# A hybrid mixer layer on one core: later adaLN columns summed on VectorE during S5's inputs, the out projection of two token blocks under the last branch, and a shorter norm chain

## The chip, the cores and the metric

The kernel runs on one core of one Trainium2 chip. The metric is the device time of one launch in microseconds (us). TensorE (PE) does matmuls, VectorE (DVE), ScalarE (ACT) and GpSimd (POOL) elementwise work, and all DMAs of this kernel are issued from SyncE's queue (SP), in that queue's order.

## What is computed

One layer of a hybrid backbone: 512 latent and 256 context tokens of width 1024. Three mixers (HGRN2, gated DeltaNet, S5) run on one norm of the input; their outputs are projected, gated, added and projected out, and an MLP follows. The six adaLN vectors `ml[0]` to `ml[5]` are columns of one product with `ada_w`. The first two are needed at the start, `ml[2]` to `ml[4]` only behind the mixers, `ml[5]` at the end. Cut to what matters:

```python
ml = split(silu(c) @ ada_w + ada_b, 6)
pl = split(modulate(rmsnorm(xl, norm1_w), ml[0], ml[1]) @ w_in, ...)
ya, yb, ycc = hgrn2(...) @ w_ba, deltanet(...) @ w_bb, s5(...) @ w_bc
xl = xl + ml[2] * ((g_a * ya + g_b * yb + g_c * ycc) @ w_o)      # g: sigmoid gates of pl
xl = xl + ml[5] * (square(relu(modulate(rmsnorm(xl, norm2_w), ml[3], ml[4]) @ w1)) @ w2)
return rmsnorm(xl, final_norm_w)
```

All is float32. A product is made of three TensorE matmuls on two parts of each operand.

## The kernel before

Each operand of a product is split into a high part `hi`, rounded by ScalarE (L225, L238), and a low part `lo`, the rest, by VectorE (L226, L239) or GpSimd; `mm3` (L245 to L248) adds three matmuls. Weights stream through `W`: half-megabyte loads into three `raw` buffers, then two buffers each of `hi` and `lo`. A load can be issued when the split of the load three before it is done. SyncE issues in order, so a DMA that waits holds up all behind it.

The code is written as generators, `weave` runs a main one and a filler by a plan, and a scheduler then lists each engine's order from the trace of the program. After that the order of each engine is fixed: a matmul that waits holds all matmuls behind it.

The stages, by the times of the profile: start and first adaLN vectors to 56 us; S5's input projection to 98; `state_in` (L338 to L374), which makes S5's inputs, to 147; the S5 scan on GpSimd from 147 on, beside HGRN2; two pairs of DeltaNet heads (545 to 705 and 717 to 905) with fillers; the rest of branch c to 945; branch b to 990; the out projection with norms to 1042; the MLP to 1395; the last norms.

`state_in` takes eight groups. Each spreads a 16-wide factor over 128 columns in six elementwise operations (L338 to L347), five of the groups on GpSimd and three on VectorE, transposes the result on TensorE (L365), copies it on ScalarE (L367), multiplies with the columns `U` (L370) and copies into the scan's state `sv` (L372 to L374). `U` is written to DRAM in `s5du` by four blocks and read back in another layout, one load for two groups.

`ada_rest(j, pool)` makes one of `ml[2]` to `ml[5]`. Eight matrices of 128x1024 are loaded into `raw`, scaled by a column of `silu(c)` on ScalarE (L1290) and added up on GpSimd (L1291). Eight matmuls of one column (L1297) sum over partitions, and VectorE adds the bias (L1298). j = 2, 3 and 4 run as fillers of the second DeltaNet pair, together with `branch("a")`; j = 5 runs in the MLP's first half.

`branch(n, ...)` goes over eight blocks of output columns: a gate, a weight block (`W.load`), 12 matmuls, `(gate + 1) * p` on VectorE (L1384), the add of the branches so far, loaded from `mg` (L1388), and `last(b, g)`. For branch b `last` splits the merged block into `gh` and `gl`. Between the blocks `resident` loads and splits one block of `w_out` with GpSimd's help. The out projection runs behind that, for four blocks of 128 tokens and two halves of columns, each into a `pj` bank of PSUM, followed by gate and residual (L1487, L1488) and `norm`. `norm` takes squares with sums on ScalarE (L1495), 13 VectorE steps on 128x1 (L1496, L1497 and `rsqrt`, L183 to L188), and the scaling of `x1` by VectorE (L1513). After transposes the modulation of eight column blocks is VectorE's (L1521).

## Time and profile before

| | |
|---|---|
| median of 3 runs | 1406.12 us (1405.9 to 1409.2) |
| profiled execution | 1412.48 us |
| its span, first to last instruction | 1410.8 us |
| busy: TensorE, VectorE, ScalarE, GpSimd | 90%, 63%, 34%, 28% of the span |
| mean granted TensorE clock | 0.956 of full speed |
| DMA | 161.31 MB, mean 114 GB/s |

The page gives busy times, the windows give them for a stretch, and the timeline gives each instruction with the idle time of its engine before it and what released it. A row names the line, the engine, the operation, the output and inputs by the program's names, and the shapes.

### The profile page before, as it was taken

What the parts mean: (1) busy time and instruction counts of PE and PEld (TensorE: products, weight loads), DVE (VectorE), ACT (ScalarE), POOL (GpSimd) and SP (SyncE); (2) the same over time, 40 slices, a digit from 0 to 9 for tenths busy, and PEclk for the clock granted to TensorE, in tenths of its full rate; (3) what the DMA queues carried; (4) which work ended last, traced back from release to release, by engine and by line L of the source; (5) the groups of instructions that cost most, each with busy time, mean ns of one, the idle gap of its engine ahead of it and who ended that gap; (6) DMA issues with size and microseconds to landing.
All of it is one profiled execution on the core that took longest, in us unless ns stands there. A gap on an engine that the chain in (4) does not pass through costs nothing. (4 is left out here: it accounts for less than half of the span.)

```text
span 1410.8 us, 18360 instructions
## 1 busy us (share of the span) xinstructions
PE 1276.2 (90%) x6829; PEld 1047.0 (74%) x6829; DVE 886.7 (63%) x1705; ACT 482.5 (34%) x879; POOL 391.1 (28%) x510
## 2 busy tenths in 40 slices
PE   7788999999998898899976889976999999999995
PEld 2367777888787786798866788754777888888884
DVE  6744487866779668897559766437766422544236
ACT  3426313433334355222252432223234422244222
POOL 0255799997005620000004630004004000000002
PEclk9898999999999899999988989989999999999998
DMA  8773442738847674924565775788226333332321
GB/s 292 122 148 55 56 62 38 110 51 66 109 65 124 74 166 129 101 46 68 117 160 183 225 151 95 161 184 245 78 60 182 117 96 98 90 105 90 105 90 61
DMA packets 182266, 161.31 MB, mean 114 GB/s; under 512 B 24800, under 2 KB 152480, under 8 KB 182176
## 3 DMA queue, kind: packets, MB, share of 16 engines
q1 hardware_dynamic: 182176, 160.14, 52.8%
q8 instruction: 54, 0.88, 0.3%
q14 instruction: 36, 0.29, 0.1%
HBM read 141.24 MB, written 18.87 MB: 113 GB/s over the span
## 5 line engine op out<-in xcount | busy, mean ns | idle before, releaser
L226 DVE TENSOR_TENSOR lo<-raw,hi 128x1024 fp32r<-128x1024 f32 (+1 forms) x161 | 189.9, 1180 | 260.2 <-ACT hi L225 259.9
L225 ACT ACTIVATE hi<-raw 128x1024 fp32r<-128x1024 f32 (+1 forms) x161 | 157.5, 979 | 398.3 <-PE pj L247 228.2
L246 PE MATMUL pj<-hh,hi 128*128 128x512 f32 (+1 forms) x520 | 216.3, 416 | 16.5 <-ACT hi L225 11.5
L248 PE MATMUL pj<-hh,lo 128*128 128x512 f32 (+1 forms) x520 | 213.8, 411 | 1.0 <-DVE lo L226 1.0
L247 PE MATMUL pj<-hl,hi 128*128 128x512 f32 (+1 forms) x520 | 213.3, 410 | 0.8 <-POOL hl L1148 0.8
L247 PE MATMUL pj<-hc,hi 128*128 128x512 f32 (+2 forms) x536 | 187.4, 350 | 1.7 <-DVE hc L239 0.8
L246 PE MATMUL pj<-h,hi 128*128 128x512 f32 (+1 forms) x304 | 117.1, 386 | 12.6 <-ACT hi L225 11.5
L246 PEld LDWEIGHTS pj<-hh,hi 128*128 128x128 f32 (+1 forms) x520 | 101.2, 195 | 35.6 <-ACT hi L225 12.5
L248 PE MATMUL pj<-h,lo 128*128 128x512 f32 (+1 forms) x304 | 116.5, 384 | 3.6 <-DVE lo L226 3.3
L247 PEld LDWEIGHTS pj<-hl,hi 128*128 128x128 f32 (+1 forms) x520 | 101.1, 194 | 21.1 <-POOL hl L1148 2.4
L248 PEld LDWEIGHTS pj<-hh,lo 128*128 128x128 f32 (+1 forms) x520 | 100.4, 193 | 21.9 <-DVE lo L226 2.1
L247 PEld LDWEIGHTS pj<-hc,hi 128*128 128x128 f32 (+1 forms) x536 | 101.9, 190 | 16.4 <-DVE hc L239 1.6
L1584 POOL TENSOR_TENSOR xn<-x,row 128x512 f32<-128x512 f32 x8 | 10.4, 1301 | 313.4 <-DVE x L1488 307.6
L246 PE MATMUL pj<-hc,hi 128*128 128x256 f32 (+2 forms) x264 | 86.0, 326 | 11.3 <-ACT hi L225 7.1
L248 PE MATMUL pj<-hc,lo 128*128 128x256 f32 (+2 forms) x264 | 84.9, 322 | 5.0 <-DVE lo L226 5.0
L1291 POOL TENSOR_TENSOR s<-s,raw 128x1024 f32<-128x1024 f32 x21 | 51.3, 2444 | 113.8 <-DMA mg<-fg 81.4
L246 PEld LDWEIGHTS pj<-h,hi 128*128 128x128 f32 x304 | 57.8, 191 | 26.5 <-ACT hi L225 14.9
L248 PEld LDWEIGHTS pj<-h,lo 128*128 128x128 f32 x304 | 57.7, 190 | 17.8 <-DVE lo L226 7.2
L246 PEld LDWEIGHTS pj<-hc,hi 128*128 128x128 f32 (+1 forms) x264 | 50.8, 193 | 15.9 <-ACT hi L225 7.5
L248 PEld LDWEIGHTS pj<-hc,lo 128*128 128x128 f32 (+1 forms) x264 | 50.7, 192 | 8.9 <-DVE lo L226 5.9
L382 POOL TENSOR_TENSOR sw<-sp,sv 128x64 f32<-128x64 f32 x94 | 50.7, 540 | 22.9 <-ACT sv L373 15.6
L239 POOL TENSOR_TENSOR act<-raw,act 128x1024 fp32r<-128x1024 f32 x8 | 19.2, 2395 | 127.0 <-ACT act L238 127.0
(535 smaller groups left out, 2760.3 us busy)
## 6 DMA issues: line engine op xcount, KB each, us to landing
raw<-in_w_in SPq DMA_DIRECT2D x72, 512.0 KB
raw<-in_w_ff SPq DMA_DIRECT2D x64, 512.0 KB
raw<-in_ada_w SPq DMA_DIRECT2D x40, 512.0 KB
dg<-fg SPq DMA_DIRECT2D x16, 256.0 KB
fg<-dg SPq DMA_DIRECT2D x16, 256.0 KB
mg<-fg SPq DMA_DIRECT2D x16, 256.0 KB
fg<-mg SPq DMA_DIRECT2D x16, 256.0 KB
raw<-in_w_out SPq DMA_DIRECT2D x8, 512.0 KB
```

Source lines behind the costliest of these rows:

```text
L225: K.nc.scalar.activation(hi, w, AF.Copy)
L226: (engine or K.nc.vector).tensor_tensor(lo, w, hi.bitcast(FT), op=OP.subtract)
L239: (engine or K.nc.vector).tensor_tensor(lo, x, hi.bitcast(FT), op=OP.subtract)
L246: nc.tensor.matmul(out, wh, xh, start=start, stop=False)
L247: nc.tensor.matmul(out, wh, xl, start=False, stop=False)
L248: nc.tensor.matmul(out, wl, xh, start=False, stop=stop)
L382: e.tensor_tensor(t[:, 1], aa[:, 1], ap(x, 96 * G, [[-96 * G, 2], [96, G]]), op=OP.mult)
L1291: nc.gpsimd.tensor_tensor(acc, acc, w, op=OP.add)
L1584: nc.gpsimd.tensor_tensor(t[:, s], x1[i][:, s], fw[:, s], op=OP.mult)
```

## The change

Three things change.

1. `ada_rest` for j = 2, 3 and 4 leaves the second pair's fillers and is run by `ada_gates` in steps of `state_in`, which is now a generator. Loads are 1 MB into the two buffers of the tag `nt`; the first matrix is scaled by ScalarE, the seven others are scaled and added by one VectorE instruction each. The column sums, the bias and the write of `drow` follow there. The last of the three runs on in `chain(mix(hgrn2_in(0), taps, ...))`. The plan and the filler list of the second pair are new.
2. The out projection of the first two token blocks is issued in `last` of branch b, for the block before, into the `tr` and `mm` banks. `w_out` goes through the two `xn` buffers instead of `raw`, and `x1` is loaded from block 4 on.
3. The norm chain has 9 steps instead of 13 (a factor of -1/256 goes into `mod2` and into the final weight), the scaling of `x1` and two in four modulations are ScalarE's. j = 5 uses a `raw` tile for each matrix and one more step.

```diff
+    def ada_rest(j, acc, fetch, engine):
+        kt = 0
+        while kt < 8:
+            two = fetch()
+            n = two.shape[1]
+            k.dma(two, ada_w[128 * kt:128 * (kt + n), 1024 * j:1024 * j + 1024].rearrange("(x p) m -> p x m", p=128))
+            for i in range(n):
+                w, c = two[:, i], cs[:, kt + i, 0:1]
+                if not kt + i:
+                    nc.scalar.activation(acc, w, AF.Copy, scale=c)
+                elif engine is v:
+                    v.scalar_tensor_tensor(acc, w, c, acc, op0=OP.mult, op1=OP.add)
+                else:
+                    nc.scalar.activation(w, w, AF.Copy, scale=c)
+                    engine.tensor_tensor(acc, acc, w, op=OP.add)
+            kt += n
+            if kt % 2 == 0:
+                yield
+        yield
...
+    def ada_gates():
+        done = iter(())
+        for j in (2, 3, 4):
+            g = ada_rest(j, k.t("s4", [128, 1024]), lambda: k.t("nt", [128, 2, 1024]), v)
+            for i in range(4):
+                next(g)
+                if i == 1:
+                    for _ in done:
+                        pass
+                yield
+            done = g
+        yield done
...
-    s5.state_in()
+    ada = ada_gates()
+    for _ in s5.state_in():
+        next(ada)
     s5.scan()
+    for last_sums in ada:
+        pass
...
-    for _ in chain(mix(hgrn2_in(0), taps), gates(0, range(0, 1))):
+    for _ in chain(mix(hgrn2_in(0), taps, last_sums), gates(0, range(0, 1))):
...
-    weave(pair(1), chain(gates(1, range(2, 3)), mix(gates(1, range(3, 5)), gates(1, range(5, 6))), mix(branch("a", w_ba, range(8), last=save(mg[0])), chain(gates(1, range(6, 8)), ada_rest(2, s4), mix(ada_rest(3, s4), ada_rest(4, s4)))), branch("c", w_bc, (), scale=0.25, prev=mg[0], last=save(mg[1]))), (7, 11), (8, 6), (8, 4), (4, 6), (21, 8))
+    weave(pair(1), chain(gates(1, range(2, 6)), mix(branch("a", w_ba, range(8), last=save(mg[0])), gates(1, range(6, 8))), branch("c", w_bc, (), scale=0.25, prev=mg[0], last=save(mg[1]))), (7, 6), (5, 4), (12, 4), (21, 4))
...
+    def merged(b, g):
+        split_act(k, gh[:, b], gl[:, b], g)
+        if b:
+            for i in range(2):
+                for h in range(2):
+                    project_out(first[i][h], i, h, b - 1)
+
+    for b, _ in enumerate(branch("b", w_bb, range(8), prev=mg[1], last=merged)):
+        wo += resident(w_out, 128 * b, 1, lambda shape: k.t("xn", shape), nc.gpsimd)
...
-        v.tensor_tensor(st[:, i, 2:3], st[:, i, 0:1], st[:, i, 1:2], op=OP.add)
-        v.tensor_scalar(st[:, i, 2:3], st[:, i, 2:3], 1.0 / 1024, EPS, op0=OP.mult, op1=OP.add)
-        rsqrt(v, st[:, i, 4:5], st[:, i, 2:3], st[:, i, 3:4])
-        return t, st[:, i, 4:5]
+        x, y, z = st[:, i, 2:3], st[:, i, 3:4], st[:, i, 4:5]
+        v.tensor_scalar(x, st[:, i, 0:1], st[:, i, 1:2], 1024 * EPS, op0=OP.add, op1=OP.add)
+        v.tensor_scalar(z.bitcast(I32), x.bitcast(I32), 1, None, op0=OP.logical_shift_right)
+        v.tensor_scalar(y.bitcast(I32), z.bitcast(I32), -1.0, 1597463007.0, op0=OP.mult, op1=OP.add)
+        for c in (3.0, 12.0, 768.0):
+            v.tensor_scalar(z, y, y, x, op0=OP.mult, op1=OP.mult)
+            v.scalar_tensor_tensor(y, z, c, y, op0=OP.subtract, op1=OP.mult)
+        return t, y
...
-        v.tensor_scalar(t, x1[i], r, None, op0=OP.mult)
+        nc.scalar.activation(t, x1[i], AF.Copy, scale=r)
```

What this does to the order of instructions is read at three places. The first is SyncE's queue in S5's inputs; `s` with the source `s5du` is a load of U, `s5du` as a target a write of it. Before:

```order
L63 DMA s_100_831<-s5du_567 128x8x96
L63 DMA s5dul<-s_98_824 1024x1x64
L63 DMA s_117_909<-s5du_568 128x8x96
L63 DMA s5du_570<-s_98_824 8x16x768
L63 DMA s_134_987<-s5du_569 128x8x96
L63 DMA s_151_1065<-s5du_570 128x8x96
L63 DMA raw_1946<-in_w_in 128x8x128
```

Now, from the third of these rows on:

```order
L62 DMA s_120_920<-s5du_568 128x8x96
L62 DMA s5du_570<-s_98_826 8x16x768
L62 DMA nt_960<-in_ada_w 128x2x1024
L62 DMA nt_1002<-in_ada_w 128x2x1024
L62 DMA s_139_1006<-s5du_569 128x8x96
L62 DMA nt_1047<-in_ada_w 128x2x1024
L62 DMA nt_1089<-in_ada_w 128x2x1024
L62 DMA drow<-r_1106 8x128
L62 DMA s_161_1109<-s5du_570 128x8x96
L62 DMA nt_1149<-in_ada_w 128x2x1024
L62 DMA nt_1191<-in_ada_w 128x2x1024
L62 DMA raw_2035<-in_w_in 128x8x128
```

The third and fourth load of U now stand behind two and four loads of 1 MB, and the fourth behind the write of `drow` too, which waits for the first column sum. VectorE in the same place, before, at its last group of `state_in`:

```order
L338 TENSOR_TENSOR s_160_1105<-sp_428,s_76_429 128x512
L339 TENSOR_TENSOR s_127_950<-sp_428,s_76_429 128x512
L341 TENSOR_TENSOR s_160_1105<-sp_428,s_76_429 128x512
L340 TENSOR_TENSOR s_126_949<-s_126_949,s_127_950 128x512
L342 TENSOR_TENSOR s_127_950<-sp_428,s_76_429 128x512
L347 TENSOR_TENSOR s_126_949<-s_126_949,s_127_950 128x512
```

Now, from the first sum of j = 3 to the end of the last group of `state_in`:

```order
L1191 SCALAR_TENSOR_TENSOR s_148_1046<-nt_1047,cs,s_148_1046 128x1024
L337 TENSOR_TENSOR s_171_1153<-sp_428,s_76_429 128x512
L340 TENSOR_TENSOR s_171_1153<-sp_428,s_76_429 128x512
L1191 SCALAR_TENSOR_TENSOR s_148_1046<-nt_1089,cs,s_148_1046 128x1024 x2
L1191 SCALAR_TENSOR_TENSOR s_148_1046<-nt_1149,cs,s_148_1046 128x1024
L338 TENSOR_TENSOR s_172_1154<-sp_428,s_76_429 128x512
L1191 SCALAR_TENSOR_TENSOR s_148_1046<-nt_1149,cs,s_148_1046 128x1024
L339 TENSOR_TENSOR s_171_1153<-s_171_1153,s_172_1154 128x512
L1191 SCALAR_TENSOR_TENSOR s_148_1046<-nt_1191,cs,s_148_1046 128x1024
L341 TENSOR_TENSOR s_172_1154<-sp_428,s_76_429 128x512
L1191 SCALAR_TENSOR_TENSOR s_148_1046<-nt_1191,cs,s_148_1046 128x1024
L346 TENSOR_TENSOR s_171_1153<-s_171_1153,s_172_1154 128x512
```

All seven sums of j = 3 stand ahead of the end of the last spread, six of them between its operations. The third place is TensorE in branch b. Before, its 12 matmuls of a block (`h` with a `hi` or `lo`) follow those of the block before, and the first matmul of the out projection (`act`, `gh`) stands in the last block:

```order
L248 MATMUL pj_8378<-h_1363_8155,lo_8375 128x512
L246 MATMUL pj_8411<-h_1363_8155,hi_8407 128x512
L247 MATMUL pj_8411<-h_1363_8155,hi_8407 128x512
L246 MATMUL pj_8450<-act_8201,gh 128x512
L247 MATMUL pj_8450<-act_8202,gh 128x512
L248 MATMUL pj_8411<-h_1363_8155,lo_8408 128x512
```

Now, at the end of one block and the start of the next:

```order
L247 MATMUL pj_8263<-h_1355_8115,lo_8260 128x512
L245 MATMUL tr_8111<-act_8251,gh 128x512
L246 MATMUL tr_8111<-act_8252,gh 128x512
L247 MATMUL tr_8111<-act_8251,gl 128x512
...
L245 MATMUL mm_8114<-act_8251,gh 128x512
L246 MATMUL mm_8114<-act_8252,gh 128x512
L247 MATMUL mm_8114<-act_8251,gl 128x512
L245 MATMUL pj_8308<-h_1355_8115,hi_8304 128x512
```

From the third block on, 12 matmuls of the out projection stand behind the 12 of each block (six of them left out in the fence).

## Rows read from the trace of the kernel before

**Rows 1.** The page, parts 1 and 5: busy time, share, count; groups.

```profile
PE 1276.2 (90%) x6829; PEld 1047.0 (74%) x6829; DVE 886.7 (63%) x1705; ACT 482.5 (34%) x879; POOL 391.1 (28%) x510
...
L226 DVE TENSOR_TENSOR lo<-raw,hi 128x1024 fp32r<-128x1024 f32 (+1 forms) x161 | 189.9, 1180 | 260.2 <-ACT hi L225 259.9
...
L1291 POOL TENSOR_TENSOR s<-s,raw 128x1024 f32<-128x1024 f32 x21 | 51.3, 2444 | 113.8 <-DMA mg<-fg 81.4
```

**Rows 2.** Windows: length, busy PE, PEld, DVE, ACT, POOL; PE clock, DMA share, GB/s.

```profile
0.00:56.00 56.00, 38.11 (x129) 11.23 (x129) 36.84 (x206) 20.15 (x40) 2.09 (x8) 0.96 0.78 247
98.00:147.00 49.00, 38.47 (x249) 33.89 (x248) 25.59 (x24) 26.81 (x68) 23.48 (x18) 0.90 0.38 67
739.00:840.00 101.00, 81.00 (x522) 73.33 (x522) 82.48 (x124) 38.40 (x46) 54.05 (x25) 0.90 0.69 189
910.00:940.00 30.00, 18.68 (x67) 14.09 (x66) 8.91 (x12) 6.53 (x10) 0.00 (x0) 0.83 0.91 184
920.00:930.00 10.00, 5.58 (x20) 4.19 (x18) 0.00 (x0) 0.00 (x0) 0.00 (x0) 0.84 0.90 70
945.00:983.00 38.00, 25.07 (x87) 17.04 (x86) 26.28 (x26) 13.86 (x21) 16.42 (x7) 0.91 0.74 229
```

**Rows 3.** Timeline of TensorE, pair 1: start, us, instruction, idle before and releaser.

```profile
746.95 0.79 PE L248 MATMUL pj<-hc,lo 128*128 128x512 f32 x1 [4.10 <-DVE lo L226]
...
789.75 1.84 PE L1297 MATMUL att<-one,s 128*128 128x1 f32 x16
...
825.99 0.50 PE L246 MATMUL pj<-hh,hi 128*128 128x512 f32 x1 [2.64 <-ACT hi L225]
```

**Rows 4.** Timeline of VectorE in pair 1, four column scalings twice.

```profile
741.95 3.15 DVE L844 TENSOR_SCALAR s<-upper,gu 128x128 f32<-128x128 f32 x4
...
751.62 1.08 DVE L844 TENSOR_SCALAR s<-upper,gu 128x128 f32<-128x128 f32 x4
```

**Rows 5.** Timeline of TensorE at the end of branch c.

```profile
917.44 0.50 PE L246 MATMUL pj<-hh,hi 128*128 128x512 f32 x1 [3.72 <-ACT hi L225]
...
932.65 0.80 PE L246 MATMUL pj<-hc,hi 128*128 128x512 f32 x1 [7.07 <-ACT hi L225]
```

**Rows 6.** Timeline of TensorE in branch b.

```profile
954.60 0.50 PE L246 MATMUL pj<-h,hi 128*128 128x512 f32 x1 [1.69 <-ACT hi L225]
...
957.27 0.39 PE L247 MATMUL pj<-h,hi 128*128 128x512 f32 x1
957.50 0.39 PE L248 MATMUL pj<-h,lo 128*128 128x512 f32 x1
...
982.81 0.50 PE L246 MATMUL pj<-h,hi 128*128 128x512 f32 x1 [1.15 <-ACT hi L225]
```

**Rows 7.** Timeline of VectorE in branch b, the merge add.

```profile
951.37 0.69 DVE L1388 TENSOR_TENSOR fg<-fg,fg 128x512 f32<-128x512 f32 x1 [2.60 <-DMA fg<-mg]
...
956.50 2.67 DVE L1388 TENSOR_TENSOR fg<-fg,fg 128x512 f32<-128x512 f32 x1 [1.24 <-DMA fg<-mg]
```

**Rows 8.** Timeline of VectorE, two steps of the last norm chain.

```profile
1403.51 0.15 DVE L1497 TENSOR_SCALAR st<-st 128x1 f32<-128x1 f32 x1
1403.70 0.15 DVE L183 TENSOR_SCALAR st<-st 128x1 int32<-128x1 int32 x1
```

**Rows 9.** Timeline of TensorE, VectorE and GpSimd in S5's inputs.

```profile
104.86 3.70 PE L370 MATMUL mm<-s,s 128*128 128x96 f32 x16 [6.01 <-DMA s<-s5du]
...
115.92 1.66 DVE L338 TENSOR_TENSOR s<-sp,s 128x512 f32<-128x512 f32 x1 [9.73 <-PE tr L365]
...
123.89 1.43 DVE L347 TENSOR_TENSOR s<-s,s 128x512 f32<-128x512 f32 x1
...
112.58 1.06 POOL L338 TENSOR_TENSOR s<-sp,s 128x512 f32<-128x512 f32 x1
...
130.09 1.60 POOL L347 TENSOR_TENSOR s<-s,s 128x512 f32<-128x512 f32 x1
...
147.26 0.35 POOL L382 TENSOR_TENSOR sw<-sp,sv 128x64 f32<-128x64 f32 x1 [15.57 <-ACT sv L373]
```

More of the change, by code (lines that the diff above doesn't have):

```diff
@@ L1174, in project @@
         return res if len(res) > 1 else res[0]
+    mod2 = consts.tile([128, 4, 8], FT, name="mod2")
+    drow = k.d("drow", [2, 1024])
+    def ada_rest(j, acc, fetch, engine):
[17 more added lines that the diff above has]
+        yield
+        m = mod2[:, j - 2]
+        p = k.p("att", [128, 8])
+        for b in range(8):
+            nc.tensor.matmul(p[:, b:b + 1], acc[:, 128 * b:128 * b + 128], k.one, start=True, stop=True)
+        v.tensor_tensor(m, p, at["ada_b"][:, 8 * j:8 * j + 8], op=OP.add)
+        if j == 4:
+            v.scalar_tensor_tensor(m, m, 1.0, at["n2"], op0=OP.add, op1=OP.mult)
+            v.tensor_scalar(m, m, -1.0 / 256, None, op0=OP.mult)
+        if j in (2, 5):
+            if j == 2:
+                v.tensor_scalar(m, m, 0.5, None, op0=OP.mult)
+            p = k.p("att", [8, 128])
+            nc.tensor.transpose(p, m, k.ident)
+            r = consts.tile([8, 128], FT, name=f"r{j}")
+            nc.scalar.activation(r, p, AF.Copy)
+            k.dma(drow[j // 3].rearrange("(b n) -> b n", b=8), r)
+        yield
+    def ada_gates():
[7 more added lines that the diff above has]
+                        pass
+                yield
+            done = g
+        yield done
     def silu2(out, p, x=None):
@@ L1473, in resident, with project_out @@
         return res
-    wo = []
-    for b, _ in enumerate(branch("b", w_bb, range(8), prev=mg[1], last=lambda b, g: split_act(k, gh[:, b], gl[:, b], g))):
-        wo += resident(w_out, 128 * b, 1, nc.gpsimd)
-    x1 = [k.t("x1", [128, 1024]) for _ in range(4)]
-    for i in range(4):
-        k.dma(x1[i], x[128 * i:128 * i + 128])
+    wo, first = [], [[k.p(n, [128, 512]) for _ in range(2)] for n in ("tr", "mm")]
+    x1 = []
+    def project_out(p, i, h, kt):
+        s, w = slice(128 * i, 128 * i + 128), slice(512 * h, 512 * h + 512)
+        mm3(nc, p, gh[:, kt, s], gl[:, kt, s], wo[kt][0][:, w], wo[kt][1][:, w], kt == 0, kt == 7)
+    def merged(b, g):
[6 more added lines that the diff above has]
+        wo += resident(w_out, 128 * b, 1, lambda shape: k.t("xn", shape), nc.gpsimd)
+        if b >= 4:
+            i = b - 4
+            x1.append(k.t("x1", [128, 1024]))
+            with k.queued(nc.sync):
+                k.dma(x1[i], x[128 * i:128 * i + 128])
+    for i in range(2):
+        for h in range(2):
+            project_out(first[i][h], i, h, 7)
     G2 = row(drow[0])
@@ L1539, in hybrid_block @@
         for f in range(16):
-            if not half and 4 <= f < 9:
+            if not half and 4 <= f < 10:
                 next(last_ada)
```

58 lines of the change are left out of this document (17 added, 41 removed).

## The prediction

> **What bounds the kernel now.** I read the page's busy shares first. TensorE is busy 90% of the span [rows 1], so what can be gained is the 10% in which it stands, and the stretches in which it runs at a lower granted clock. The windows [rows 2] say where these are: each gives TensorE's busy time, its granted clock (as a share of 2.4 GHz) and the DMA share. What the diff touches are four stretches: 98 to 147 us (S5's inputs, 38.47 busy of 49), 739 to 840 (second pair of DeltaNet heads, 81.00 of 101), 910 to 940 (last blocks of branch c, 18.68 of 30) and 945 to 983 (branch b, 25.07 of 38). For each I then read TensorE's timeline for the idle time before a matmul and its releaser, and the releaser's engine beside it. The profiled execution took 1412.48 us (span 1410.8 and 1.7 around it), and the median of the runs is 6.4 below that. The sum is made on 1412.5, and 6.4 is taken off at the end.
>
> **Pair 1: 24 loads, 24 scales on ScalarE, 21 adds on GpSimd and 48 one-column matmuls leave.** Between 739 and 830 us TensorE has six gaps of over 0.8 us, 19.1 us together; the first and the last are in [rows 3], three are of 4 us or more. Most wait for VectorE, which is busy 82.48 of 101 us there [rows 2]. [Rows 4] show why it is late: four column scalings of 128x128 take 3.15 us while GpSimd adds, and 1.08 us when it doesn't. There are 21 such adds of 2.44 us [rows 1], and all leave. What can come back is the 19.1 us of gaps; the low clock, 81.00 x (1 - 0.90) = 8; and three batches of 16 column sums of 1.84 us [rows 3], 5.5. Together 33. I don't take all of it. Some 5 us of the gaps are the pair's own chain, since its VectorE steps at their undisturbed length still stand between two batches of matmuls. Another 5 or 6 go because the clock falls again wherever a gap of a few us stays, and because the filler list has the same matmuls of branch a for the whole pair. Taken: **22**, bounds 8 (column sums and a little clock) and 30.
>
> **End of branch c.** Two gaps of 3.72 and 7.07 us [rows 5] stand ahead of matmuls that wait for ScalarE's split of a weight block, and that waits for its load: the DMA share is 0.91 [rows 2]. With the low clock (18.68 x 0.17 = 3.2) that is 14. The 24 loads of pair 1 no longer hold the three raw buffers, so branch c's weights can be asked for earlier. But in the order of after, half-megabyte loads of w_out stand between those of branch c, and they come to a DMA that is full. Taken: **4**, bounds 0 and 12.
>
> **Branch b and out projection.** Branch b's blocks start 5.6 us apart (five blocks between the first two rows of [rows 6]) for 12 matmuls of 0.23 us pitch, 2.8 us. The gaps, seven with 12.8 us in all (the second and the last are in the rows), wait for ScalarE's weight split. In ScalarE's queue that split stands behind the copy of a merged block, which waits for VectorE's merge add L1388. This add takes 2.67 us beside a GpSimd split of w_out and 0.69 without, and it waits for a load itself [rows 7]. After the change 96 matmuls of the out projection (22 us) stand between branch b's, and need nothing but the block before. They lie in the gaps. 12.8 us of gaps, two of 0.8 where the two streams mix now, and the low clock (25.07 x 0.09 = 2.3) make 16.7. The splits of w_out come earlier, beside branch c. A block then has 24 matmuls, 5.5 us, against a chain of up to 5.6, so some waits stay. Taken: **13**, bounds 0 and 17.
>
> **Norm chain.** 13 small VectorE steps at 0.19 us start to start [rows 8] become 9, 0.8 us for each of four blocks. Three lie under matmuls of the next block. The fourth's delays the MLP's first columns, and the last chain of the kernel lies bare at its end. With the normalise step and half of the modulation on ScalarE: **2**, bounds 0.5 and 4.
>
> **What the move costs in S5's inputs.** It brings 12 loads of 1 MB and 21 multiply-adds of 128x1024 on VectorE. No row shows that instruction; VectorE's subtract of the same shape takes 1.18 us [rows 1]. In the order of after 14 of them stand ahead of the end of VectorE's last spread. The spreads run on VectorE and GpSimd together, and [rows 9] show what that does: a 128x512 product on VectorE takes 1.66 us (an add of that shape alone 0.69 [rows 7]), on GpSimd 1.06 alone. From 115.92 to 125.32 six VectorE operations ran and some six and a half of GpSimd: alone 4.1 and 6.9, 11.0 together, done in 9.4. So two busy engines need 0.85 of their sum. The sum for this stage is GpSimd 18 x 1.06 = 19.1 and VectorE 18 x 0.69 + 16 x 1.18 = 31.3, together 50.4; by 0.85, 43 us from 98: the last spread would end at 141. Before, the same working gives 34 x 0.85 = 29, 127, and the last one ended at 131.7 [rows 9]: 5 us were waits. So 146, and some 5 for the last group's transposes, matmuls and copies: 151. With 4 us of waits for the loads I take 155 for the start of S5's scan, not 147.26 [rows 9]: **8**. Without any mutual delay, VectorE's 31 us alone would end at 129 and the cost would be 0.
> The Trainium skill, "SBUF — State Buffer", section "Who interferes with whom", says that a VectorE instruction with two SBUF inputs and a GpSimd instruction that reads SBUF exclude each other, the later one blocked for the whole instruction. By that rule the factor would be 1, the last spread 7 us later and this cost 15; the 9.4 us for 11.0 lie between exclusion and freedom, nearer to exclusion.
> The loads are the other price. 6.3 MB must land between the last write of U (about 105 us, where the first matmul behind U starts [rows 9]) and VectorE's last spread, on the queue that also brings U. At the rate of the start, 247/0.78 = 317 GB/s at full share, that takes 20 us; at this stage's 67/0.38 = 176 it takes 36, until 141, just under the 146. TensorE's fillers stand in a fixed order among S5's matmuls, so the delay is TensorE's. S5's scan has room behind it: the page's slices show GpSimd idle for some 70 us there. Two of the loads stand ahead of the last first-stage weights, 0 to 2 us, taken 1. The third column sum stands in a full stretch, 1.8. The late sums lie under projections, on a VectorE that is busy half of the time. Cost **11**, bounds 3 (no mutual delay) and 20.
>
> **Sum.** 22 + 4 + 13 + 2 - 11 = 30. 1412.5 - 30 = 1382.5 for a profiled execution, **1376** for the median.
>
> **Rivals.**
> *Half stays (26%).* Either pair 1's gaps are its own chain of VectorE and TensorE steps, and that part gives 8; or branch b's chain of load, add, copy and split doesn't shrink and the new matmuls add to it (a pitch of 5.6 + 2.8), and that part gives 0. For it: VectorE's 82.48 us of 101 are mostly the pair's own work, and the merge add waits for a load [rows 7]. Against it: the stretched rows [rows 4, 7]. Either way 16 or 17 stay: **1390**.
> *All of it (17%).* Pair 1 gives 30 and branch c's end 12, since the raw buffers were the cause: 46, **1360**. Against it: the DMA share of 0.91.
> *Slower (6%).* The loads crawl as the DMA did from 920 to 930, 70 GB/s at a share of 0.90, thus 78: 6.3 MB take 81 us, to 186, VectorE's last sums and spread end at 188, the scan starts at 192, 45 late. With 2.8 for start and column sum that costs 48 against gains of 41: 7 slower, **1413**. It decides from a cost of 41, at rates below some 85 GB/s. For it: U is moved in rows of 384 bytes in this very stretch, on the same queue. Against it: 176 at full share in this stage.
> *Nothing (3%).* Both halves stay away and the move costs its 20: 8 + 4 + 0 + 2 - 20 = -6, and with a little less of the cost within 0.3%: **1408**.
>
> **How the numbers follow.** Forecast 48%, all 17, half 26, slower 6, nothing 3. A measurement can tell about 0.3%, 4.2 us, from no change. The range takes in the full and the half case with some of their bounds, and leaves out the slow ones: 1357 to 1396. Faster is forecast, all and half, 0.91, less 0.02 for a half case with a dear S5 stage: 0.89. Same 0.05, slower 0.06.
>
> **What would show it.** S5's scan should start at 150 to 160. A start past 170 with VectorE waiting for a DMA is the slow rival. Pair 1's four scalings should be near 1.08 us, and gaps of 4 to 5 us gone; if these stand with their releaser unchanged, the share for the adds was wrong. Branch b's blocks should come every 5.5 to 6 us with 24 matmuls; 8 us means the chain. If the gaps from 910 to 940 go, the raw buffers were the cause and not the DMA.

## The result, and the profile after

| | before | after |
|---|---|---|
| median of 4 runs each | 1407.66 us (1405.9 to 1409.4) | 1393.65 us (1392.3 to 1394.1) |
| profiled execution, its span | 1412.48, 1410.8 | 1393.29, 1391.6 |
| mean granted TensorE clock | 0.956 | 0.963 |

The change makes the kernel faster, by a ratio of 0.9899 [0.9881, 0.9917], 14 us. The forecast was 30 us, 1376. So the direction held and the size did not. (One of the ten runs of the kernel with the third part alone, below, took 2473.58 us; medians are over all runs, ratios leave it out.) The page after, part 1 (busy time, share, count; before in [rows 1]), and the groups of the new instruction and of the column sums:

```profile
PE 1269.6 (91%) x6829; PEld 1042.0 (75%) x6829; DVE 888.4 (64%) x1675; ACT 470.4 (34%) x878; POOL 358.0 (26%) x490
...
L1191 DVE SCALAR_TENSOR_TENSOR s<-nt,cs,s 128x1024 f32<-128x1024 f32 x21 | 31.1, 1481 | 22.8 <-ACT s L1189 11.5 <-DMA nt<-in_ada_w 11.0
...
L1202 PE MATMUL att<-one,s 128*128 128x1 f32 x48 | 6.0, 255 | 0.9 <-DVE s L1191 0.9
```

TensorE's busy time fell by 6.6 us only. The span fell by 19, so most of the gain is idle time. To see where it lies I read, from TensorE's timeline of both profiled executions, the first or last matmul of each stage:

| stage, us | before | after | gain | forecast |
|---|---|---|---|---|
| to the end of the first stage, 56 | 56.0 | 55.0 | 1.0 | 0 |
| S5's inputs and scan, to the first HGRN2 chunk | 172.3 | 194.7 | -22.4 | -11 |
| HGRN2 | 321.2 | 315.5 | 5.7 | 0 |
| pair 0 | 157.0 | 155.7 | 1.3 | 0 |
| pair 1 | 169.3 | 144.2 | 25.1 | 22 |
| rest of branch c | 69.4 | 73.2 | -3.8 | 4 |
| branch b, out projection, norms, MLP's first product | 186.8 | 178.7 | 8.1 | 13 and 1 |
| MLP's second product | 262.4 | 262.5 | -0.1 | 0 |
| last norms | 16.3 | 12.1 | 4.2 | 1 |
| span | 1410.8 | 1391.6 | 19.2 | 30 |

(The 2 us of the norm chain are divided here between the two stages that have it.) HGRN2's code is untouched, and over kernels in which it is the same its length ran from 314 to 324 us in the profiled executions below. Its 5.7 us are spread, not gain. The stage of S5 spreads less: seven kernels below and above with the old code in it take 171.3 to 172.3 us, and five with the new code (the change, part 1 alone and the last three kernels below) 191.8 to 194.7, mean 192.9. So the move costs 20 to 22 us, the changed kernel's own execution is the longest of the five, and a difference of under 3 us in this stage is not shown by one execution. The windows after, on the stretches of [rows 2] as far as they moved (length, busy PE, PEld, DVE, ACT, POOL, PE clock, DMA share, GB/s):

```profile
98.00:159.00 61.00, 45.80 (x289) 40.62 (x290) 38.94 (x36) 27.13 (x66) 29.20 (x18) 0.85 0.70 186
159.00:251.00 92.00, 88.50 (x563) 66.76 (x562) 68.58 (x93) 21.60 (x35) 85.79 (x153) 0.95 0.43 81
...
739.00:840.00 101.00, 94.75 (x593) 82.76 (x592) 83.07 (x157) 22.59 (x57) 2.48 (x4) 0.95 0.43 98
910.00:940.00 30.00, 20.27 (x79) 15.77 (x79) 15.16 (x10) 7.83 (x10) 10.12 (x4) 0.83 0.82 205
945.00:983.00 38.00, 37.29 (x156) 30.12 (x156) 22.71 (x30) 10.76 (x16) 5.01 (x3) 0.96 0.74 234
1020.00:1030.00 10.00, 3.51 (x14) 2.89 (x15) 5.31 (x16) 5.90 (x11) 0.00 (x0) 0.58 0.19 54
```

Pair 1 and branch b are now nearly full: 94.75 of 101 and 37.29 of 38, against 81.00 and 25.07. Branch c's end is as empty as it was, and there is a new hole at 1020, where TensorE works 3.51 of 10 us. The scan's counterpart of the last of [rows 9], then VectorE's scalings and TensorE's waits in pair 1 (start, us, instruction, idle before it and releaser):

```profile
159.25 0.36 POOL L382 TENSOR_TENSOR sw<-sp,sv 128x64 f32<-128x64 f32 x1 [13.30 <-ACT sv L372]
```

```profile
753.60 1.11 DVE L844 TENSOR_SCALAR s<-upper,gu 128x128 f32<-128x128 f32 x4
```

```profile
731.92 0.79 PE L245 MATMUL pj<-hc,hi 128*128 128x512 f32 x1 [9.02 <-ACT hc L237]
...
767.28 1.62 PE L878 MATMUL mm<-s,nt 128*128 128x128 f32 x6 [3.96 <-DVE s L883]
```

The scan starts at 159.25, inside the 150 to 160 that I gave as the mark of the forecast. The scalings take 1.11 us, and of the six gaps of over 0.8 us only the 3.96 is left behind 739. (The 9.02 stands earlier in the pair, where the kernel before waits 2.96 and 4.24 us.) Both marks were right, and yet the stage of the first cost twice the forecast: it goes on behind the mark.

### The profile page after: what moved, and what is told of

Same layout as the page of the kernel before. It is cut to its first block, busy times and chain, and to the rows that moved or that the text cites. A ratio compares the mean times of both kernels' runs of the same rounds, so it can differ in the third digit from the quotient of the medians.

```text
span 1391.6 us, 18282 instructions
## 1 busy us (share of the span) xinstructions
PE 1269.6 (91%) x6829; PEld 1042.0 (75%) x6829; DVE 888.4 (64%) x1675; ACT 470.4 (34%) x878; POOL 358.0 (26%) x490
## 4 chain that ended last, share of the span: by engine, by line
PE 63%; DVE 13%; DMA 12%; issue 3%; ACT 3%; POOL 1%; SPq 0%; POOLq 0%; DVEq 0%; ACTq 0%
PE pj L245 13%; PE pj L247 13%; PE pj L246 13%; DMA nt<-in_ada_w 3%; PE mm L878 2%; PE mm L887 2%; PE att L552 2%; DVE lo L225 2%; DMA raw<-in_w_in 2%; DMA xn<-in_w_out 1%; PE tr L247 1%; DVE s L1191 1%; PE tr L245 1%; PE tr L246 1%; DMA fg<-na 1%
## 5 line engine op out<-in xcount | busy, mean ns | idle before, releaser
L225 DVE TENSOR_TENSOR lo<-raw,hi 128x1024 fp32r<-128x1024 f32 (+1 forms) x161 | 194.1, 1207 | 230.5 <-ACT hi L224 230.2
L1004 POOL TENSOR_SCALAR_AFFINE_SELECT s<-s 128x512 f32<-128x512 f32 x8 | 5.9, 755 | 298.8 <-DVE s L832 88.8
L384 POOL TENSOR_TENSOR sw<-sw,sv 128x64 f32<-128x64 f32 x94 | 52.7, 561 | 0.0
L382 POOL TENSOR_TENSOR sw<-sp,sv 128x64 f32<-128x64 f32 x94 | 47.1, 501 | 20.6 <-ACT sv L372 13.3
```

Source lines behind the costliest of these rows:

```text
L225: (engine or K.nc.vector).tensor_tensor(lo, w, hi.bitcast(FT), op=OP.subtract)
L382: e.tensor_tensor(t[:, 1], aa[:, 1], ap(x, 96 * G, [[-96 * G, 2], [96, G]]), op=OP.mult)
L384: e.tensor_tensor(t[:, 1], t[:, 1], y, op=OP.add)
```

## The experiments

Kernels ran in four groups, each with its own runs of the kernel before on the same chip, and a ratio is to those. The medians of before there were 1408.36, 1411.00, 1409.79 and 1411.65 us. "Stage" means a row of the table above, from each kernel's profiled execution. Every diff is cut to its main lines.

### The three parts apart

Four kernels are the kernel before with one or two of the three parts of the change: the sums moved (part 1), the out projection under branch b (part 2), the norm chain (part 3), and parts 2 and 3 together.

> The kernel before with the first part of the change alone: the sums of ml[2] to ml[4] on VectorE in S5's inputs, and the new plan of the second DeltaNet pair. Theory 1 (read from the two traces, matmul by matmul: TensorE is 20 us later at 300 us than before, 14.6 later when the pair begins and 9 earlier behind it): the S5 scan starts at 157 to 161 us instead of 147, the pair gives back 22 to 25, and alone this part gains 7 to 11 us. Rival (my forecast): it costs 11 and gives 22 plus 4 at the end of branch c, so 13 to 17 us are gained.

> The kernel before with the second part alone: the out projection of token blocks 0 and 1 under branch b, w_out through the xn buffers, x1 later. Theory 1: branch b's gaps are filled (12 to 14 us), but the norm chains of four token blocks, some 10 us each and one behind the other, then have only two blocks of matmuls above them, so TensorE waits 7 to 10 us for the last one: 3 to 7 us gained. Rival (my forecast): what is filled under branch b comes out at the end, 12 to 14 us gained.

> The kernel before with the third part alone: 9 steps in the norm chain, normalise and half of the modulation on ScalarE. Theory 1: the bare end of the kernel gets 3 to 5 us shorter (TensorE's last matmul to the end was 16.7 us before and 12.5 after) and nothing else moves, since TensorE hardly waited for a norm chain in the middle. Rival (my forecast): 1 us in the middle and 1 at the end.

> The kernel before with the second and third part and without the first. Theory 1: 3 to 7 of the out projection, 3 to 5 of the end, and a last norm chain that is 1 to 2 us shorter where it lies bare: 8 to 13 us gained. If the whole change is the sum of its parts, this and the first part alone add up to the 14 us measured; if the end of branch c is made worse only by both (w_out's loads asked for in a fuller queue), they add up to more.

| | median, us | ratio | S5's inputs and scan | pair 1 | rest of c | branch b to MLP | last norms |
|---|---|---|---|---|---|---|---|
| part 1 | 1402.47 | 0.9938 [0.9913, 0.9963] | 192.1 | 146.4 | 70.8 | 186.7 | 15.2 |
| part 2 | 1410.35 | 1.0003 [0.9982, 1.0025] | 172.0 | 169.1 | 73.1 | 180.9 | 15.5 |
| part 3 | 1407.27 | 0.9988 [0.9968, 1.0007] | 171.4 | 168.8 | 70.0 | 186.0 | 12.3 |
| 2 and 3 | 1401.36 | 0.9932 [0.9907, 0.9957] | 171.5 | 169.9 | 73.2 | 178.2 | 12.2 |

Some 20 us lost in S5's stage and 23 won in pair 1 come with part 1 alone, the 4 us lost at branch c's end and the 6 us won in branch b with part 2 alone, and the 4 us at the end with part 3. By their ratios, part 1 gives 8.7 us and parts 2 and 3 give 9.6, 18 together against 14 for the whole; the intervals, some 3.5 us to either side, cover that. Part 1 came as its theory said (the scan at 158.38 us, 22.9 in the pair, 8.7 in all), and part 3 too. Parts 2 and 3 don't add up so well: alone they give -0.4 (3 to 7 were expected) and 1.7 us by their ratios, together 9.6. In the three stages that they touch, the profiled executions have 3.0, 4.2 and together 8.9. Why the medians of the two alone stay below that, no run shows.

### What the sums cost in S5's inputs

The rival causes are the sums on VectorE, the twelve loads, the column sums on TensorE, and the buffer ring that the sum tiles share with the spreads (the tag `s4`). Each kernel is the changed kernel with one of them taken away.

Sums in two tiles of another tag:

```diff
-            g = ada_rest(j, k.t("s4", [128, 1024]), lambda: k.t("nt", [128, 2, 1024]), v)
+            g = ada_rest(j, [k.t("fg", [128, 512]) for _ in range(2)], lambda: k.t("nt", [128, 2, 1024]), v)
```

> The whole change, but each running sum lies in two tiles of the tag fg (unused at that time) instead of one of the eight of the tag s4; each multiply-add is thus two of 128x512. Theory A: the price in S5's inputs comes from the ring s4: GpSimd's spread at 127 us waited 6.0 us for the column sums that free a sum's tile, and those for VectorE's sums and the second pair of loads. With the sums out of the ring S5's scan starts before 152 us (159 with the change, 147 before), and 6 to 10 us of the 16 lost before the first DeltaNet pair come back. Rival B: VectorE and GpSimd together simply have too much to do there; then the scan starts at 157 to 161 as with the change and the time stays.

Sums of 8 columns:

```diff
-                    v.scalar_tensor_tensor(acc, w, c, acc, op0=OP.mult, op1=OP.add)
+                    v.scalar_tensor_tensor(acc[:, 0:8], w[:, 0:8], c, acc[:, 0:8], op0=OP.mult, op1=OP.add)
```

> The whole change with VectorE's 21 multiply-adds cut to 8 of 1024 columns; all 12 loads of 1 MB, the column sums and the waits stay (most of three of the adaLN vectors is thus left out of the result). Rival B (VectorE's work is the price): the scan starts at 147 to 150 us and 12 to 16 us of the 16 come back. Theory A (ring and loads): the waits for tiles and loads stay in part, the scan starts at 152 to 156, and 4 to 8 come back.

One pair of matrices, loaded once and held in one `nt` tile:

```diff
-            k.dma(two, ada_w[128 * kt:128 * (kt + n), ...
+            if engine is not v or (j, kt) == (2, 0):
+                k.dma(two, ada_w[128 * kt:128 * (kt + n), ...
```

> The whole change with 1 of the 12 loads of 1 MB; all multiply-adds read that one tile (11 of 12 pairs of the weights are thus left out of the result). Rival C (the loads are the price, on the queue that also brings U): the scan starts at 147 to 150. Rival B (VectorE's work): it starts at 155 to 160, by the sum of VectorE's and GpSimd's lengths. Theory A: 150 to 155, since the ring still waits for the sums, but these start earlier.

One column sum for each vector instead of eight:

```diff
-        for b in range(8):
+        some = 8 if j == 5 else 1
+        for b in range(some):
```

> The whole change with one column-sum matmul instead of eight for each of ml[2] to ml[4], its result taken for all eight columns (so seven eighths of these three vectors are wrong by that). The first chunk of the first HGRN2 head begins at 228 us before and at 248 to 250 with the change. Theory D (an account over the windows from 56 us to there: TensorE stands 7.6 us longer, loses 6.5 us more at a lower granted clock, and does 48 one-column matmuls in 6.0): their own time comes back, and with it part of the clock that falls where short waits and one-column matmuls follow each other: it begins at 239 to 243, and the clock of 178 to 188 us (0.57 to 0.58 in its slow part with the change) is full. Rival: only their own time comes back, 243 to 245, and the clock stays.

| | ratio | scan starts | stage |
|---|---|---|---|
| before | | 147.26 | 172.3 |
| after | 0.9899 [0.9881, 0.9917] | 159.25 | 194.7 |
| sum tiles apart | 0.9986 [0.9963, 1.0009] | 166.58 | 195.3 |
| sums left out | 0.9873 [0.9842, 0.9904] | 150.17 | 185.0 |
| loads left out | 0.9930 [0.9903, 0.9958] | 159.03 | 190.7 |
| column sums cut | 0.9875 [0.9852, 0.9898] | 155.37 | 190.0 |

Sums out gives back 9.7 us of the stage, loads out 4.0, column sums out 4.7; against the mean of 192.9 it is 7.9, 2.2 and 2.9. Only the first is clear of the spread, the other two lie 1 to 2 us below the shortest of the five. No single one is the cause: without the sums the scan is nearly on time, as one theory said, and yet less comes back than the 12 to 16 us that it gave.

The scan is late mostly by VectorE's sums. Without them it starts at 150.17, with the loads still there. Without the loads it starts at 159.03, as with them; but TensorE's clock from 98 to 159 was 0.77 in that execution, not 0.85, so a share of the loads may be hidden in it. The kernel with the tiles apart missed its question: the scheduler put the loads of `ada_w` ahead of U's writes, and TensorE waited for U, 12.44 us where it is 6.31 with the change. (Its first stage, too, ended at 58.7 instead of 55.0, so its total says little.) From that matmul to the scan it took 49.8 us, against 55.1 with the change (104.20 to 159.25) and 42.4 before. The 5.3 us between the first two are no measure of the ring: 20 of that kernel's 42 half sums stand ahead of the matmul, where the change has 3 of 21, and between the matmul and the scan its sums take VectorE 13.59 us instead of 17.77, which is 4.2 of them. In the changed kernel GpSimd's spread at 127.33 waits 6.01 us for the first column sums, which free a tile of the ring; whether that moves the scan is not shown. TensorE at the first U, of the kernel with the tiles apart and of the changed one:

```profile
116.83 3.48 PE L369 MATMUL mm<-s,s 128*128 128x96 f32 x15 [12.44 <-DMA s<-s5du]
```

```profile
104.20 3.70 PE L369 MATMUL mm<-s,s 128*128 128x96 f32 x16 [6.31 <-DMA s<-s5du]
```

The other 10 us lie behind the scan's start, where I had assumed cover. There the kernel before runs at 80.06 busy of 81 us and a clock of 1.00 (its window, first below); the changed one has 88.50 of 92 at 0.95. Its third batch of column sums is here, and the second row shows what comes with it: TensorE waits 0.86 us, works through one-column matmuls for 2.30, and then its clock falls to 0.66 over ten us in which it is never idle. The rows after it show the two levels: matmuls 0.43 us apart up to 184.99 (1.2 GHz), 0.23 apart from 185.41 (2.4 GHz).

```profile
147.00:228.00 81.00, 80.06 (x536) 60.35 (x535) 56.12 (x78) 19.00 (x31) 75.26 (x143) 1.00 0.40 56
```

```profile
177.13 2.30 PE L1202 MATMUL att<-one,s 128*128 128x1 f32 x16 [0.86 <-DVE s L1191]
...
184.56 0.63 PE L247 MATMUL pj<-hh,lo 128*128 128x512 f32 x1
184.99 0.58 PE L245 MATMUL pj<-hh,hi 128*128 128x512 f32 x1
185.41 0.39 PE L246 MATMUL pj<-hl,hi 128*128 128x512 f32 x1
185.63 0.40 PE L247 MATMUL pj<-hh,lo 128*128 128x512 f32 x1
```

```profile
178.00:188.00 10.00, 10.00 (x39) 7.81 (x39) 7.27 (x12) 1.55 (x2) 9.37 (x17) 0.66 0.50 72
```

Over the whole stretch from 98 the account closes within a microsecond. Idle time: 10.5 before and 15.2 after up to the scan, 0.9 and 3.5 behind it, +7.3. Low clock (busy time times one less the clock): 3.8 and 6.9, none and 4.4, +7.5. Column sums: 6.0. Together 20.8, against 21.5 by which the first HGRN2 chunk is late. Cutting the column sums alone gave back 3 to 5 us, their own time or less, as the rival said, and left a clock of 0.83 in the same ten us, with waits of 1.52 and 3.30 us on TensorE just before and in them; so a lowered clock there does not need the column sums.

The loads act behind the scan too, through SyncE's queue. With the sums left out its rows (start, time in the queue for all loads of the row together, load, count), ScalarE's wait for a weight and TensorE's are:

```profile
155.42 0.37 SPq L62 DMA_DIRECT2D nt<-in_ada_w  x1
158.05 0.35 SPq L62 DMA_DIRECT2D nt<-in_s_c  x1
158.45 11.93 SPq L62 DMA_DIRECT2D raw<-in_w_in  x3
```

```profile
166.22 1.06 ACT L224 ACTIVATE hi<-raw 128x1024 fp32r<-128x1024 f32 x1 [12.35 <-DMA raw<-in_w_in]
```

```profile
167.60 0.69 PE L1273 MATMUL tr<-ident,pst 128*128 128x128 f32 x2 [5.35 <-ACT pst L1270]
```

The scan is 3 us late at most, and the weights behind the last loads into `nt` tiles are later: SyncE issues only these two between 152.7 and 158.4. 13 of the 22 us stay although VectorE has next to nothing to add.

### The same sums in another place

If the place is the trouble, the sums should cost less where nothing waits for VectorE. This kernel has the two steps on the norm chain that are told below, `state_in` as before, and each vector's sums along one filler of HGRN2, through the weights' buffers (one of three such lines):

```diff
+    sums = lambda j: ada_rest(j, s4(), lambda: W.tile([128, 1, 1024]), v)
-    chain(hgrn2_in(2), mix(context(1), scalars_in()))
+    along(chain(hgrn2_in(2), mix(context(1), scalars_in())), sums(2))
```

> As the last kernel, but the sums of ml[2] to ml[4] run on VectorE beside the fillers of the second, third and fourth HGRN2 heads (about 240 to 460 us), each matrix in one raw buffer, and S5's inputs are as before. Theory (the price of the move is its place: VectorE and GpSimd share the work of S5's inputs, and the loads hold up the projections' weights there): the scan starts at 146 to 148 again; VectorE is busy 73% of the HGRN2 stretch and the three column sums cost 5.5 us, so 6 to 11 of the 16 us lost before the first DeltaNet pair come back, and the kernel gains 22 to 28 us on the one before. Rival (three raw buffers are too few for both streams): projections wait for weights as they did at the second pair, and nothing comes back, or it is slower than the last kernel.

It took 1434.98 us, 1.0178 [1.0161, 1.0194]; the kernel with the two steps and without this move took 1391.76 in the same group. S5's stage is back at 171.8 and pair 1 stays at 145.5, but HGRN2 takes 380.8. So the rival's outcome came; its cause, the three `raw` buffers, is only a part of it. SyncE (first fence), ScalarE, VectorE and TensorE:

```profile
396.81 3.96 SPq L62 DMA_DIRECT2D raw<-in_ada_w  x2
414.91 1.64 SPq L62 DMA_DIRECT2D raw<-in_w_in  x2
```

```profile
412.56 1.06 ACT L224 ACTIVATE hi<-raw 128x1024 fp32r<-128x1024 f32 x1 [14.77 <-DMA raw<-in_w_in]
```

```profile
413.65 1.23 DVE L225 TENSOR_TENSOR lo<-raw,hi 128x1024 fp32r<-128x1024 f32 x1 [12.76 <-ACT hi L224]
```

```profile
416.89 1.09 PE L610 MATMUL tr<-ident,s 128*128 128x128 f32 x4 [14.69 <-DVE s L634]
```

SyncE issues no load between 400.8 and 414.9, and the two issued last were of `ada_w`, so two of the three buffers are theirs. But the weight that ScalarE, VectorE and TensorE stand for had its load issued before, at 395.54. From 400 to 408 us the DMA engines were busy 0.98 to 1.00 of the time and moved 37 and 52 GB/s: this load was under way and came slowly. How much of the 61 us is buffers and how much is DMA, no run takes apart. The 22 us of the chosen place are cheap beside this.

### What freed pair 1

The kernel before, with the adds on GpSimd cut to 8 columns, and a second one with the column sums cut as well. Loads and scales stay in both.

```diff
-                nc.gpsimd.tensor_tensor(acc, acc, w, op=OP.add)
+                nc.gpsimd.tensor_tensor(acc[:, 0:8], acc[:, 0:8], w[:, 0:8], op=OP.add)
```

> The kernel before with GpSimd's 21 adds under the second DeltaNet pair cut to 8 of 1024 columns; loads, scales on ScalarE, column sums and plan stay (most of three adaLN vectors is left out of the result). With the change the stretch from the pair's first matmul to its last takes 144 to 147 us, before 169. My step (the adds stretch VectorE, and VectorE holds TensorE): the stretch falls to 152 to 159, 10 to 17 of the 24 come from the adds. Rival (the 24 loads in the three raw buffers, and the scales and column sums, are what costs): it stays within 4 us of 169.

> The kernel before with GpSimd's adds cut as in the run of the cut adds, and one column-sum matmul instead of eight. The second DeltaNet pair took 169.3 us before, 157.7 with the adds cut, 144 to 147 with the change. Theory: 5 to 8 of the 12 left are the column sums; the stretch takes 150 to 153, and the rest is loads, scales and the new plan. Rival: the rest of the gain is loads and scales on the three raw buffers, and it stays at 155 to 158.

They took 1397.27 (0.9925 [0.9899, 0.9951]) and 1392.81 (0.9869 [0.985, 0.9887]). The pair takes 157.7 and 155.0 us, from 169.3 before and towards 144.2 with the change. So GpSimd's adds are 11.6 of the 25, the column sums 2.7 more, where I expected 5 to 8; the rival's 155 to 158 held. (Over the kernels here the pair takes 168.8 to 169.9 us with the old code and 143.2 to 146.4 with the new, so the 2.7 are near the spread.) The 10.8 that are left belong to the loads, the scales on ScalarE and the new plan of fillers, which no run here takes apart.

### The norm chain behind branch b

With the change TensorE's last long wait ahead of the MLP, and the starts of the last two norm chains on VectorE, are:

```profile
1024.90 1.97 PE L1570 MATMUL tr<-ident,xn 128*128 128x128 f32 x8 [5.70 <-ACT xn L1566]
```

```profile
1011.07 0.21 DVE L1543 TENSOR_SCALAR st<-st 128x1 f32<-128x1 f32 x1 [0.85 <-ACT t L1541]
...
1016.00 1.43 DVE L1578 TENSOR_SCALAR t<-tr,mod 128x128 f32<-128x128 f32 x4 [2.24 <-ACT t L1576]
...
1021.57 0.21 DVE L1543 TENSOR_SCALAR st<-st 128x1 f32<-128x1 f32 x1 [0.85 <-ACT t L1541]
```

The chains start 10.5 us apart, since VectorE takes the residual of a block only behind the modulation of the one before, and that waits 2.24 us for ScalarE's half. If this is the bound, issuing the next block's residual and norm ahead of the modulation should take the wait away. A second kernel also splits the MLP's columns so that the last block's come in two pieces.

```diff
+    ts = [residual(0)]
+    for i in range(4):
+        if i < 3:
+            ts.append(residual(i + 1))
+        modulated(i, ts[i])
```

```diff
-    for s in (slice(0, 256), slice(256, 512)):
+    for s in (slice(0, 256), slice(256, 384), slice(384, 512)):
```

> The whole change, but gate, residual, squares and norm chain of token block i + 1 are written ahead of the transposes and the modulation of block i. Theory: with two blocks of the out projection under branch b, four norm chains of 10.2 us each, one behind the other, bound the stretch from 988 to 1029 us, and TensorE waits 5.70 and 1.59 us for the last one; with the next block's chain begun during this one's modulation they take some 7.5 each, the wait of 5.7 goes and 5 to 8 us are gained against the change. Rival: the last chain alone is what TensorE waits for; nothing changes (within 2 us).

> The kernel with the residual written ahead, and the MLP's first columns done in tokens 0 to 255, 256 to 383 and 384 to 511 instead of two halves, so that 48 matmuls of 128 columns need only the third block's norm. Theory: what is left of the wait for the last norm chain (b's start to the MLP's second product 174.0 us with the residual ahead, 178.7 with the change) falls by 2 to 3 us. Rival: the narrower matmuls cost as much as they cover, within 1 us.

The stage went from 178.7 to 174.0 and 172.7, and the first of them shows (TensorE):

```profile
1022.63 1.09 PE L1573 MATMUL tr<-ident,xn 128*128 128x128 f32 x8 [0.20 <-ACT xn L1565]
...
1025.84 0.64 PE L245 MATMUL pj<-h,hi 128*128 128x256 f32 x2 [2.12 <-ACT h L237]
```

5.70 became 0.20, of which 4.7 reached the end of the stage. Six kernels without this edit take 178.2 to 181.2 us there, so the 174.0 is clear of the spread, and the 1.3 of the thirds (2 to 3 were expected) is not. The medians, 1393.89 (0.9874 [0.9839, 0.9909]) and 1391.76 (0.9874 [0.9853, 0.9895]), are too near to the changed kernel's to show it: their intervals overlap. The evidence is the stage.

### The end of branch c

After the change TensorE, ScalarE and SyncE show at branch c's end:

```profile
923.67 0.80 PE L245 MATMUL pj<-hc,hi 128*128 128x512 f32 x1 [7.61 <-ACT hi L224]
```

```profile
922.04 1.06 ACT L237 ACTIVATE act<-xn 128x1024 fp32r<-128x1024 f32 x1 [13.07 <-DMA xn<-in_w_out]
923.01 0.61 ACT L224 ACTIVATE hi<-raw 128x512 fp32r<-128x512 f32 x1
```

```profile
906.47 3.44 SPq L62 DMA_DIRECT2D xn<-in_w_out  x1
910.79 3.36 SPq L62 DMA_DIRECT2D xn<-in_w_out  x1
914.19 2.38 SPq L62 DMA_DIRECT2D raw<-in_w_bc  x1
```

Branch c's load is behind two loads of `w_out` on SyncE, and its split is behind a split of `w_out` on ScalarE. Theory: without them the end shrinks to 69 or below; rival: the DMA is full anyway, and it stays at 73. The kernel is the one before it (norm ahead, thirds) with the loads of `w_out` kept in the order of the program:

```diff
+                with k.queued(nc.sync):
+                    k.dma(t, w[r0 + 128 * kt:r0 + 128 * kt + 128, :])
```

> The kernel with the residual ahead and the thirds, but the loads of w_out keep their place in the program behind branch b's earlier loads, so none stands between branch c's loads. From the second pair's end to branch b's first matmul it takes 69 to 71 us in kernels without the out projection under branch b and 73 to 75 with it. Theory: w_out's loads on the full queue are the 3.5 us; the stretch takes 69 to 71 again. What it may cost: w_out comes later, the out projection's matmuls slip behind branch b, and the stretch from branch b to the MLP's second product (172.7) grows by as much or more.

1387.09 us, 0.9820 [0.9795, 0.9844]: the fastest kernel here, 25 us below the kernel before. The rest of c takes 67.6 instead of 73.2, and the stage behind it 174.0, 1.3 longer than without this edit, which is within the spread. The window and the wait that is left:

```profile
910.00:940.00 30.00, 22.12 (x80) 16.20 (x80) 11.23 (x16) 8.07 (x13) 0.00 (x0) 0.89 0.77 143
```

```profile
928.90 0.60 PE L245 MATMUL pj<-hh,hi 128*128 128x512 f32 x1 [3.33 <-ACT hi L224]
```

7.61 became 3.33, and the clock 0.89 instead of 0.83. The DMA did not get faster: in the changed kernel it moves 44 GB/s at a share of 0.94 from 910 to 915, and here 44 and 42 GB/s at 0.93 and 1.00 from 915 to 925. What changed is the order: a load of `w_bc` is issued at 906.77, where the changed kernel has two of `w_out`, and ScalarE splits that block at 916.62, as the stretch begins.

## Why the prediction was right, and where it was not

**Pair 1, forecast 22, measured 25.** The size was right and its account half right. Without the adds alone the pair gains 11.6, so they are the largest cause that was measured alone, as the stretched scalings [rows 4] told. I put the column sums at 5.5 inside it, and they gave 2.7. I took the fillers' plan to hold the pair back by 5 or 6; about 11 us more came with the loads, the scales and that plan together.

**S5's inputs, forecast 11 lost, measured 21.5** (22.4 in the table, less the 1.0 by which the first stage ends earlier). The failing step is "The late sums lie under projections", with the first two batches of column sums, and any loss of clock, costed at nothing. The delay of the scan was 12 against 8, the smaller part of the miss, and the working behind the 8 has two wrong readings. It took 131.7 for the end of the last spread before. That is GpSimd's; VectorE's ended at 141.58, behind a weight split that had waited 6.80 us for ScalarE. VectorE, before and after:

```profile
139.76 1.23 DVE L226 TENSOR_TENSOR lo<-raw,hi 128x1024 fp32r<-128x1024 f32 x1 [6.80 <-ACT hi L225]
140.90 0.68 DVE L347 TENSOR_TENSOR s<-s,s 128x512 f32<-128x512 f32 x1
```

```profile
149.42 0.68 DVE L346 TENSOR_TENSOR s<-s,s 128x512 f32<-128x512 f32 x1
```

So the working, which gives 127, left 14 us of the kernel before unexplained and not 5, and that its 155 came near 159.25 is partly luck. Of the 12 us, 8.5 are the last spread's (VectorE is busy all of 140 to 150), and 3.5 lie between it and the scan, where a batch of column sums of 1.87 us now stands at 154.05. The other reading is the 1.18 us: it is the mean of a group with two shapes, the subtract of 128x1024 alone has 1.28, and the new instruction took 1.48. The larger part of the miss is the stretch behind the scan, where a TensorE without a gap and at full clock (the window from 147 to 228 above) got waits, a batch of column sums and a lower clock, 9.5 us in all. The loads, which I priced by bytes up to the scan (1 us), cost little there and 2 to 4 us of the stage. The slow rival did not come: the loads' 186 GB/s at a share of 0.70 are far from 78.
The Trainium skill, "SBUF — State Buffer", section "Who interferes with whom", has a VectorE instruction with two SBUF inputs and a GpSimd instruction that reads SBUF exclude each other. With the factor of 1 that follows from it, the working of the prediction would give 158 as an estimate without any wait for a load, and the run without the loads had 159.03. But that 158 holds the 5 us of the wrong row, as does the 151 of my 0.85, so the times of the scan don't test the factor. The rows of the kernel before still show a delay short of full exclusion: by their share of that stretch 6.2 and not 6.5 operations of GpSimd ran in the 9.4 us, 10.7 us of work alone, a factor of 0.88.

**End of branch c, forecast 4 won, measured 4 lost.** The step that failed is the one that put the bounds at 0 and 12, though the order showed the loads of `w_out` between branch c's. I reckoned them as bytes on a full DMA, and left out their place in two queues: they stand 6.8 us on SyncE ahead of branch c's load, and ScalarE splits them ahead of branch c's weight. Keeping them back removes both and gave 5.6 back; which of the two counts more is not shown.

**Branch b and the norm chains, forecast 13 and 1, measured 8.** The step itself held. TensorE's idle time from 945 to 983 went from 12.9 to 0.7 us, and blocks come every 5.45 us (958.25 to 980.05, four blocks) where I gave 5.5 to 6. (My 5.6 for the kernel before is read between the first and the last of [rows 6].) What failed is "Three lie under matmuls of the next block": with half of the out projection gone from behind branch b, the 96 matmuls left there (22 us) no longer cover four norm chains that start 10.5 us apart, and 5.70 us of wait came up at the last. With the residual ahead the stage gains 12.8, and 14.1 with the thirds.

**Last norms, forecast 1, measured 4.2.** I saw one bare chain, the last, and it shortened as I said: from its first step to the scaling 2.97 us before (1402.91 to 1405.88), 2.19 after (1385.28 to 1387.47). But the last block's gate on VectorE stands behind the chain of the block before. TensorE's last matmul ends at 1394.45 before and 1379.48 after, and that gate starts 6.3 and 3.3 us later. VectorE, before and after:

```profile
1400.71 0.68 DVE L1487 TENSOR_TENSOR t<-tr,row 128x512 f32<-128x512 f32 x1
...
1402.91 0.57 DVE L1496 TENSOR_TENSOR st<-st 128x1 f32<-128x1 f32 x1 [0.79 <-ACT t L1495]
...
1405.88 0.49 DVE L1586 TENSOR_SCALAR xn<-xn,st 128x512 f32<-128x512 f32 x1
```

```profile
1382.81 0.68 DVE L1533 TENSOR_TENSOR t<-tr,row 128x512 f32<-128x512 f32 x1
...
1385.28 0.21 DVE L1543 TENSOR_SCALAR st<-st 128x1 f32<-128x1 f32 x1 [0.79 <-ACT t L1541]
...
1387.47 0.49 DVE L1644 TENSOR_SCALAR xn<-xn,st 128x512 f32<-128x512 f32 x1
```

Two chains lay on the path where I costed one, and the first of them was worth 2.9 us.

**The 6.4 us taken off.** They were the profiled execution's distance from the median before. The profiled execution after was at its own median (1393.29, 1393.65), so this was the spread of one run and no constant. It made 6.8 of the 17.7 us by which 1376 was too low. The stages made the other 10.8: misses of 10.5 in S5's inputs, 7.8 at branch c's end and 6 in branch b with the norms, less 3 of pair 1, 3 of the tail and some 7 by which the untouched stages were shorter in this execution.

**The rivals.** The time fell near the 1390 of "half stays", but by neither of its mechanisms: both halves came, and what was left went elsewhere.

## What to carry to other kernels

Try a working on the kernel before first: where it is 14 us short there, a mark that it nearly hits afterwards proves little. A mark such as "the scan starts at 155" bounds the cost of a move only up to the mark: reckon also the stretch behind it, with its idle time, its clock and the queue that the moved loads share. A moved load is two queue entries, its own and that of the operation that consumes it; find what stands behind both. Where waits are filled with work taken from a later stage, look at what that work covered there, since its cover leaves with it.

## What the runs showed of the hardware

- A wait of 0.86 us and a batch of sixteen one-column matmuls were followed by 6 us at 1.2 GHz with TensorE busy all the time (179 to 185 us). In the last three kernels above the same batch stands behind waits of 0.75 to 1.12 us, and 3 to 6 us of matmuls at 1.2 GHz follow too, as behind 2.24 us in the kernel with the tiles apart; in part 1 alone it has no wait ahead of it, and the clock is 1.00 over the same ten us. Two other batches of the changed kernel without a wait ahead, at 125.41 and 1077.01, kept the clock.
- A multiply-add of 128x1024 on VectorE takes 1.27 us undisturbed and 2.07 beside GpSimd; these two rows are 3.7 us apart in the changed kernel:

```profile
118.12 2.07 DVE L1191 SCALAR_TENSOR_TENSOR s<-nt,cs,s 128x1024 f32<-128x1024 f32 x1
...
121.79 1.27 DVE L1191 SCALAR_TENSOR_TENSOR s<-nt,cs,s 128x1024 f32<-128x1024 f32 x1
```

- The DMA engines can be busy and slow for some 5 to 10 us at a time: 43 GB/s at a share of 0.95 before (920 to 925 us), 44 at 0.94 after (910 to 915), where the first 56 us before have 247 at 0.78. In the kernel with the sums beside HGRN2's fillers a load issued at 395.54 was there for ScalarE only at 412.56, over such a stretch.
- The same code of HGRN2 took 314 to 324 us in different executions, and the kernel before 1402 to 1419 over all its runs. A gain of 5 us in one stage of one profile is therefore shown only with the wait that left beside it.
